# A decoder layer's split token rows, key rows and fourth weight pool at other places modulo 256 bytes

## The chip, the core and the metric

The kernel runs on one core of a Trainium2 chip. The core has a matrix engine (TensorE, "PE" in the profile, with its weight loads on a row of their own, "PEld"), a vector engine (VectorE, DVE), a scalar engine (ScalarE, ACT), a general engine (GpSimd, POOL) and a queue engine that issues transfers (SyncE, SP). The on-chip memory (SBUF) has 128 partitions; an address in this document is a byte offset within a partition. The metric is the device time of one execution in microseconds; the median of several runs is compared.

## What is computed

One decoder layer over 4096 prompt tokens and 64 sample tokens, width 1024, in float32. It has one input projection, three head groups and one output projection:

```python
h = _rmsnorm(x, g_pre)
z = h @ w_in                                    # 1024 x 2816
cb, cc, ch, cg, q, k, v, ag, mq, mg = _split_cols(z)
out_a = silu(cg) * cb * conv3(cc * ch)          # gated short convolution, 256 channels
out_b = silu(ag) * window_attention(q, k, v, sink)   # 8 heads, window 128
out_c = silu(mg) * memory_attention(mq, mk, mv)      # 4 heads, 256 memory tokens
y = concatenate([out_a, out_b, out_c]) @ w_out
return x + _rmsnorm(y, g_post)
```

Keys, values, convolution rows and memory keys and values are outputs too.

## The kernel before

**Products in parts.** The matrix unit multiplies in a reduced-width float32 form (float32r). To keep float32 accuracy each operand is split: `hi` is the operand rounded to that form, `lo` the remainder. A product is then three matmuls, weights-hi times rows-hi, weights-hi times rows-lo, weights-lo times rows-hi. `product` (L368) does this for four slices of 128 inputs, so twelve matmuls of line 373 per product, each with a stationary 128 x 128 slice `w[:, 0 or 1, ks]` and a moving row of 260 tokens, `h[0][:, k]` (hi) or `h[1][:, k]` (lo).

**The input projection.** The 4160 token rows are cut into 8 blocks of 2 x 260 tokens (`NBLK`, `HW`). Blocks are done with Strassen-like products, seven per 2 x 2 partition (`PRODUCTS`), apart from the first two of the first phase, which are done plainly with eight (`plain_block`). There are three phases (`PHASES`), with four pairs of weight columns in the first two and three in the last. `input_projection` (L924) runs over `steps` = (phase, block, product); while one step multiplies, `h_split(i + 1)` prepares the next rows: `split` (L361) writes the hi tile with ScalarE (L363) and the lo tile with VectorE (L364). Accumulators in PSUM are evicted by `evict` (L376 to L395), mostly on VectorE at L380. In the trace the plain blocks and phase 0 last to about 350 us, phase 1 to about 670, phase 2 to about 926, and window and memory attention with the output projection from there to the end.

**Order.** Phase 0 is under a manual schedule; in the later phases the program order is kept for chosen instructions. Matmuls run in program order on TensorE.

**Where tiles lie.** Tiles come from pools on a left stack that grows up and a right stack that grows down. For this document the residue modulo 256 counts, and the sizes below are bytes per partition. In the program of before the pools start at:

| pool | holds | address | modulo 256 |
|---|---|---|---|
| `wa` | weights of pairs 0 to 2, later `w_out` and the split `mix` | 20,704 | 224 |
| `wb` (right) | weights of pair 3 in phases 0 and 1 | 200,672 | 224 |
| `hp` | two hi and two lo tiles | 131,680 | 96 |
| `bq` | queries of even chunks | 115,040 | 96 |
| `keys` | keys of even chunks (`kst`) | 147,808 | 96 |
| `pre` (right) | queries of odd chunks, then their keys | 195,744 | 160 |
| `memkv` (right) | memory keys `mk` first | 215,200 | 160 |

A weight tile takes 4096 bytes (parts 2048 apart, slices 512 apart). A split tile takes `KH` = 4 rows with a pitch of `XR` = 320 elements, 1280 bytes, so 5120 in all; 260 of the 320 elements are used, and `begins` (L354) says at which element the used part starts: 48 for hi and 16 for lo. Hence hi rows start at 96 + 192 = 288, place 32, and lo rows at 96 + 64, place 160, in every tile.

In attention `kst` has four rows of 384 elements (1536 bytes) per chunk of 256 tokens, hi and lo of two key heads, and `mk` has two parts of 1024 elements. Line 1253 multiplies queries (stationary) with `kst` (moving, 256 columns), line 1189 queries with `mk`, and line 1499 the split `mix` (stationary) with `w_out` (moving, 512 columns, in `wa` too; the last block's second half has 256).

Steps that the change and the working touch: `begins` and `split_tile` (L354 to L359), `wb` (L87), `place` (L90), `third_start` (L731: `mk`, `mrows`), `input_projection` (L924), `open_attention` (L1012), `load_keys` (L1108), `sample_window` (L1374).

Of the kernel before, what the change touches and what calls it, by code (L numbers as in the profile page):

```python
# [8 lines left out]
F32 = mybir.dt.float32  # L9
F32R = mybir.dt.float32r  # L10
# [5 lines left out]
P = 128  # L16
# [6 lines left out]
NT = 4096 + NS  # L23
HW = 260
XR = 320
NBLK = NT // (2 * HW)
CT = 256
NCH = 4096 // CT
# [14 lines left out]

PHASES = (((8, 9), (14, 15), (16, 17), (12, 13)), ((0, 1), (2, 3), (4, 5), (6, 7)), ((10, 11), (18, 19), (20, 21)))
PLAIN_BLOCKS = 2


def f(ap):
    return ap.bitcast(F32)
# [3 lines left out]
def hybrid_layer(ctx: ExitStack, tc: tile.TileContext, a: dict):  # L53
# [30 lines left out]
    wa = ctx.enter_context(tc.tile_pool(name="wa", bufs=3 * NP_))  # L84
    pa = ExitStack()
    wb_stack = ExitStack()
    wb = wb_stack.enter_context(tc.tile_pool(name="wb", bufs=NP_, side="right"))  # L87
    psa = ExitStack()

    place = ctx.enter_context(tc.tile_pool(name="place", bufs=1)).tile([P, 2, KH, HW], F32, name="place")  # L90
    hxp = pa.enter_context(tc.tile_pool(name="hx", bufs=4))
    hp = pa.enter_context(tc.tile_pool(name="hp", bufs=2))
    own = ExitStack()
# [257 lines left out]
                tc.keep_in_program_order(ins)  # L351
            store(hd[b][o], ops[o])

    begins = {"hi": 48, "lo": 16}  # L354

    def split_tile(tag, name):

        n = begins[tag]
        return hp.tile([P, KH, XR], F32R, tag=tag, name=name)[:, :, n : n + HW]  # L359

    def split(src, name):  # L361
# [343 lines left out]
    idle = accumulator(1, 2, "idle")  # L705
    warm = hp.tile([P, KH, XR], F32R, tag="lo", name="warm").rearrange("p k n -> p (k n)")
    G.memset(f(warm[:, : P + 512]), 1.0)
# [18 lines left out]
    right = ctx.enter_context(ExitStack())  # L726
    mem_stack = ExitStack()
    mss = const.tile([P, 4], F32, name="mss")
    third = {}

    def third_start():  # L731
        keep = right.enter_context(tc.tile_pool(name="memkv", bufs=1, side="right"))
        third["mk"] = keep.tile([P, 2, 4, 256], F32R, name="mk")
        third["mkv"] = keep.tile([P, 2, 512], F32, name="mkv")

        third["vt"] = keep.tile([P, P], F32, name="vt")
        sink, nsink = (keep.tile([P, 8], F32, name=n) for n in ("sink", "nsink"))
        third["sink"], third["nsink"] = sink, nsink
        wmask = third["wmask"] = keep.tile([P, 2, P], U8, name="wmask")
        negs = third["negs"] = keep.tile([P, 2, P], F32, name="negs")  # L740
        tc.keep_in_program_order(DMA.dma_start(sink, a["sinks"].partition_broadcast(P)))
        V.tensor_scalar(nsink, sink, -1.0, None, op0=ALU.mult)
        tc.keep_in_program_order(DMA.dma_start(negs, a["wmask"]))
        G.tensor_copy(wmask, negs)  # L744
        G.memset(negs, NEG)
        third["pre"] = right.enter_context(tc.tile_pool(name="pre", bufs=1, side="right"))

        third["parts"] = third["pre"].tile([P, 12, CT], F32, tag="q", name="mparts").rearrange("p (a b) n -> p a (b n)", a=6)
        third["mrows"] = third["pre"].tile([P, 4, P + CT], F32, tag="k", name="mrows").rearrange("p a n -> p (a n)")
        third["mem"] = mem_stack.enter_context(tc.tile_pool(name="mem", bufs=3, side="right"))  # L750
        tc.keep_in_program_order(DMA.dma_start(gmem, a["gmem"]))

# [169 lines left out]
        DMA.dma_start(third["gpost"], a["gpost"].partition_broadcast(P))  # L922

    def input_projection():  # L924
        for i, (ph, b, p) in enumerate(steps):
            if ph > 0 and b == 0 and p == 0:
                h_split(i + 1)
                for fn in pending.pop(i, ()):
                    fn()
                flush()  # L930
                in_order.close()
                store_queue[0] = DMA
                own.close()
                if ph == 2:
                    kept_z.close()
                    wb_stack.close()
                open_phase(ph)
                if ph == 2:
                    third_start()
            quads = range(len(PHASES[ph]))  # L940
            flush()
            h_load(i + 3)
            if ph == 0 or b > 0 or p > 0:
                h_split(i + 1)
            jobs = list(pending.pop(i, ()))
            if ph < 2 and p < 3:
                jobs.insert(0, lambda: t_sum(ph, b, f"T{p + 2}"))
            if ph < 2:
                jobs += next_block(ph, b, p)
            if (ph, b, p) == (0, last, 2):  # L950
                jobs.append(us_load)
            if ph == 2:
                jobs += third_jobs(b, p)
            if (ph, b) in sums_at and p in (2, 3, 4):
                jobs.append(lambda pair=sums_at[ph, b], k=p - 2: w_sums(pair, k, sums_to[pair]))
            if i > 0 and steps[i - 1][0] == 1 and steps[i - 1][1] == NBLK - 1:

                o = PRODUCTS[steps[i - 1][2]][0]
                for q in range(len(PHASES[2])):
                    load, fill = lambda q=q, o=o: next_load(2, q, o), lambda q=q, o=o: next_fill(2, q, o)  # L960
                    if o in ("S4", "A22"):

                        pending.setdefault(i + 1, []).append(load)
                        pending.setdefault(i + 3, []).append(fill)
                    else:
                        jobs.append(load)
                        pending.setdefault(i + 1, []).append(fill)
            if ph == 2 and b == last:
                for j in ((0, 1, 2), (3, 4), (5, 6, 7), (8, 9, 10, 11), (12, 13, 14, 15), (), ())[p]:
                    jobs.append(lambda j=j: wo_load(j))  # L970
                    pending.setdefault(i + (3 if j in (10, 11) else 2), []).append(lambda j=j: wo_split(j))
                if p == 1:
                    pending.setdefault(i + 1, []).append(gains_load)
                if p == 4:
                    jobs.append(blocks[0].split)
            if (ph, b, p) in SWITCH:
                jobs = SWITCH[ph, b, p]() + jobs
            if p == 0:
                zz[b] = [[None, None] for _ in quads[::2]]
            done = 0  # L980
            for q in quads:
                w = min(2, len(quads) - q // 2 * 2)
                if q % 2 == 0:
                    if p < 2:
                        zz[b][q // 2][1 - p] = z_tile(w, f"z{ph}_{b}_{q}_{1 - p}")
                    acc = accumulator(i, w, f"c{ph}_{b}_{q}_{p}")
                product(ws[ph, q, PRODUCTS[p][0]], hs[i], acc[:, q % 2])
                if q % 2 == w - 1:
                    evict(p, acc, *zz[b][q // 2])
                upto = len(jobs) * (q + 1) // len(quads)  # L990
                for fn in jobs[done:upto]:
                    fn()
                done = upto
            mem_sum()
            if p == NP_ - 1:
                z_done((0, 2, 1, 3) if ph == 1 else (2, 3, 0, 1) if ph == 0 else (1, 0))
            if p >= 5:
                ends = finish(ph, b, zz[b], p - 5)
                now = 2 if ph == 0 and b < NBLK - 1 else 1 if ph == 1 and b == 0 else len(ends)
                pending.setdefault(i + 1, []).extend(ends[:now])  # L1000
                pending.setdefault(i + 2, []).extend(ends[now:])
        for i in sorted(pending):
            for fn in pending[i]:
                fn()
        flush()
# [6 lines left out]
    def open_attention():  # L1012
# [8 lines left out]
              for tag in ("s", "t", "z", "pv")}  # L1021
# [2 lines left out]
        bq = att.enter_context(tc.tile_pool(name="bq", bufs=1))  # L1024
        places = {tag: att.enter_context(tc.tile_pool(name=tag, bufs=1 if tag == "yn" else 2))
                  for tag in ("sm", "p", "yn", "pt", "pv")}
        keys = att.enter_context(tc.tile_pool(name="keys", bufs=1))
        places["xpt"] = att.enter_context(tc.tile_pool(name="xpt", bufs=2))
        bp = {"k": keys, "vT": att.enter_context(tc.tile_pool(name="vT", bufs=1)), "q": bq}
# [9 lines left out]
    att = ctx.enter_context(ExitStack())  # L1039
# [57 lines left out]
    class Chunk:  # L1097
# [10 lines left out]
        def load_keys(self):  # L1108
            c, t0 = self.c, self.t0

            self.kst = self.pool("k").tile([P, 4, P + CT], F32R, tag="k", name=f"kst{c}")
            lo = P if c == 0 else 0
            if c == 0:
                G.memset(f(self.kst[:, :, 0:P]), 0.0)
# [258 lines left out]

    def sample_window():  # L1374
        zs = third["zs"]
        keys = bp["k"].tile([P, 4, P + CT], F32, tag="k", name="skc").rearrange("p a n -> p (a n)")
        kc = keys[:, : NB * P].rearrange("p (b k) -> p b k", b=NB)
        qb = keys[:, NB * P :].rearrange("p (b c) -> p b c", b=NB)
        DMA.dma_start(kc, a["cwk"])
# [9 lines left out]
        G.memset(neg, NEG)  # L1389
        tc.keep_in_program_order(V.tensor_scalar(scol[:, 1:2], scol[:, 0:1], -1.0, None, op0=ALU.mult))  # L1390
        yield
        values = third["pre"].tile([P, 4, P + CT], F32, tag="k", name="svc").rearrange("p a n -> p (a n)")
        vc = values[:, : NB * P].rearrange("p (b k) -> p b k", b=NB)
        DMA.dma_start(vc, a["cwv"])
        vn = vp.tile([P, P], F32, tag="v", name="svn")[:64]
# [294 lines left out]
```

## Time and profile before

| | |
|---|---|
| median of 3 runs | 1532.0 us (1529.85 to 1535.95) |
| profiled execution | 1529.03 us |
| its span, first to last instruction | 1527.3 us |
| granted TensorE clock | 1.00 |
| PE busy | 1514.2 us (99%) |
| DVE, ACT, POOL busy | 75%, 53%, 25% |

The page's fourth part follows the work that ended last back to the start:

```profile
PE 87%; DVE 5%; issue 4%; DMA 2%; POOL 1%; ACT 1%; SPq 0%; ACTq 0%; POOLq 0%; DVEq 0%
PE c L373 47%; PE y L1499 23%; PE ws L1253 4%; PE wo L1095 2%; PE wt L1276 2%; PE xs L1189 2%; PE xt L1204 2%; PE wo L1225 2%; PE wo L1231 1%; PE mem_acc L796 1%; DVE z L380 1%; DMA ws10A<-in_w_in 1%; DMA vd<-v 1%; DMA place<-hd_B 0%; DMA ws20A<-in_w_in 0%
```

In such rows "c" is an accumulator, L373 the line, and the share is that of the span. A timeline row has its start in us, its length, engine, line, operation, tiles (written tile, arrow, read tiles), the shape and a count where like instructions are merged. In tile names digits of phase and block are partly left out: `hi_6B` is a hi tile of a block 6, `w_3S` a weight tile of pair 3.

### The profile page before, as it was taken

Reading aid. Unit: us, or ns where it says so; the run is one execution under the profiler, and the core shown is the slowest. Engines: PE = TensorE matmul, PEld = TensorE weight load, DVE = VectorE, ACT = ScalarE, POOL = GpSimd, SP = SyncE. Lnnn points to the kernel's source line nnn. Section 1 sums busy time; section 2 is a strip of 40 time slices with the busy share of each in tenths; the row PEclk is TensorE's granted clock in tenths of the full one; section 3 lists DMA queues with packets and bytes.
Section 4 is the critical chain, followed back from the end, with each engine's and each line's share of the span. In section 5 each row is a group of like instructions: output and inputs, shape, how many; then the busy total and the mean of one; then the engine's idle time right before and its main releaser. Section 6 shows DMA issues by size and latency. Waiting matters only on the chain.

```text
span 1527.3 us, 30150 instructions
## 1 busy us (share of the span) xinstructions
PE 1514.2 (99%) x11331; PEld 1391.6 (91%) x11331; DVE 1145.1 (75%) x2055; ACT 806.2 (53%) x2039; POOL 381.0 (25%) x604
## 2 busy tenths in 40 slices
PE   9999999999999999999999999999999999999998
PEld 9999999999999999999999998788888888888876
DVE  6778888899887777997677678766666666666743
ACT  7776666576222222445455457656655565565632
POOL 0222333221300000000101204544444444444310
PEclk9999999999999999999999999999999999999999
DMA  9989999878755333778877789977777777776333
GB/s 274 200 213 242 286 277 259 301 238 273 194 182 181 127 127 127 240 231 278 243 262 224 242 286 259 226 160 149 149 148 152 162 149 158 162 155 145 131 110 97
DMA packets 177943, 306.28 MB, mean 201 GB/s; under 512 B 33926, under 2 KB 107654, under 8 KB 177766
## 3 DMA queue, kind: packets, MB, share of 16 engines
q1 hardware_dynamic: 130901, 227.38, 48.2%
q0 software_dynamic: 46176, 75.92, 24.9%
q8 instruction: 90, 1.47, 0.4%
q10 hardware_dynamic: 720, 1.05, 0.2%
q14 instruction: 56, 0.45, 0.1%
HBM read 197.23 MB, written 108.05 MB: 200 GB/s over the span
## 4 chain that ended last, share of the span: by engine, by line
PE 87%; DVE 5%; issue 4%; DMA 2%; POOL 1%; ACT 1%; SPq 0%; ACTq 0%; POOLq 0%; DVEq 0%
PE c L373 47%; PE y L1499 23%; PE ws L1253 4%; PE wo L1095 2%; PE wt L1276 2%; PE xs L1189 2%; PE xt L1204 2%; PE wo L1225 2%; PE wo L1231 1%; PE mem_acc L796 1%; DVE z L380 1%; DMA ws10A<-in_w_in 1%; DMA vd<-v 1%; DMA place<-hd_B 0%; DMA ws20A<-in_w_in 0%
## 5 line engine op out<-in xcount | busy, mean ns | idle before, releaser
L1499 PE MATMUL y<-wo,mh 128*128 128x512 f32 (+1 forms) x1040 | 350.1, 399 | 0.0
L380 DVE TENSOR_TENSOR z<-c,z 128x520 f32<-128x520 f32 (+1 forms) x308 | 194.8, 647 | 80.7 <-PE c L373 79.0
L1499 PEld LDWEIGHTS y<-wo,mh 128*128 128x128 f32 x1040 | 194.3, 188 | 39.3 <-issue 2.4
L1499 PE MATMUL y<-wo,ml 128*128 128x512 f32 (+1 forms) x520 | 201.8, 388 | 0.0
L1266 ACT ACTIVATE sm<-sm,wnm 128x128 f32<-128x128 f32 x256 | 99.5, 390 | 60.9 <-DVE wnm L1260 60.0
L1198 POOL TENSOR_SCALAR xp<-xp,xrd 128x256 f32<-128x256 f32 x128 | 74.6, 590 | 208.0 <-DVE xrd L1194 207.1
L1499 PEld LDWEIGHTS y<-wo,ml 128*128 128x128 f32 x520 | 98.2, 189 | 16.2
L1190 DVE TENSOR_REDUCE xmx<-xs 128x2 f32<-128x512 f32 x64 | 44.1, 689 | 59.3 <-PE xs L1189 59.2
L1278 ACT COPY wpt<-wt 128x512 f32<-128x512 f32 x64 | 37.2, 582 | 87.7 <-PE wt L1276 85.2
L1253 PEld LDWEIGHTS ws<-kst,q 128*128 128x128 f32 x512 | 70.0, 190 | 5.4 <-ACT xp L1193 0.7
L1506 DVE TENSOR_TENSOR yn<-y,gpost 128x512 f32<-128x512 f32 (+1 forms) x66 | 45.1, 684 | 39.6 <-PE y L1499 39.3
L1253 PE MATMUL ws<-kst,q 128*128 128x256 f32 x512 | 73.1, 283 | 0.4 <-ACT xp L1193 0.4
L1507 ACT ACTIVATE y<-y 128x512 f32<-128x512 f32 (+1 forms) x66 | 38.5, 584 | 64.2 <-DVE yn L1506 64.2
L744 POOL CAST wmask<-negs 128x256 uint8<-128x256 f32 x1 | 0.8, 822 | 265.2 <-ACT z L382 265.2
L1286 POOL TENSOR_SCALAR_AFFINE_SELECT wpt<-wpt 128x512 f32<-128x512 f32 x64 | 52.7, 823 | 42.0 <-ACT wpt L1278 39.1
L1193 ACT ACTIVATE xp<-xs,xnm 128x256 f32<-128x256 f32 x128 | 58.9, 464 | 7.1 <-DVE xnm L1191 7.1
L1128 POOL DMA_DIRECT2D q<-qd x64 | 42.8, 674 | 70.2 <-DMA qd<-zh 60.2
L1117 POOL DMA_DIRECT2D kst<-qd x64 | 38.7, 617 | 63.7 <-PE xt L1204 41.5
L1517 DVE SCALAR_TENSOR_TENSOR xr<-yn,yst,xr 128x1024 f32<-128x1024 f32 (+2 forms) x34 | 43.1, 1269 | 14.6 <-POOL yst L1513 13.2
L1256 DVE COPY_PREDICATED sm<-wmask,ws 128x256 f32<-128x256 uint8 x124 | 52.1, 436 | 2.4 <-ACT sm L1255 2.0
L1283 POOL TENSOR_SCALAR_AFFINE_SELECT wpv<-wpt 128x512 f32<-128x512 f32 x62 | 40.5, 653 | 50.6 <-ACT wpt L1278 50.5
L275 ACT ACTIVATE nat<-nat 104x1024 f32<-104x1024 f32 x40 | 42.3, 1057 | 18.5 <-DMA nat<-in_x_p 18.5
(962 smaller groups left out, 5076.2 us busy)
## 6 DMA issues: line engine op xcount, KB each, us to landing
q<-qd POOLq DMA_DIRECT2D x64, 384.0 KB, 8.3
xr<-in_x_p SPq DMA_DIRECT2D x32, 512.0 KB
nat<-in_x_p SPq DMA_DIRECT2D x39, 416.0 KB
o_yp<-xr SPq DMA_DIRECT2D x31, 512.0 KB
md<-th POOLq DMA_DIRECT2D x48, 260.0 KB, 7.2
qd<-zh SPq DMA_DIRECT2D x48, 260.0 KB
qd<-z SPq DMA_DIRECT2D x48, 260.0 KB
kst<-qd POOLq DMA_DIRECT2D x60, 192.0 KB, 5.5
```

Of the source, the lines that this page charges most:

```text
L373: TE.matmul(bank[:, :HW], l, r, start=first and i == 0, stop=last and i == 3 * KH - 1)
L380: add = lambda dst, other: V.tensor_tensor(dst, c, other, op=ALU.add)
L1190: V.tensor_reduce(mx[:, :nb], s, axis=AX.X, op=ALU.max)
L1193: S.activation(p[:, i, :], s[:, i, :], AF.Exp, bias=nm[:, i : i + 1], scale=SCALE, accum_out=den[:, i : i + 1])
L1198: G.tensor_scalar(p[:, i, :], p[:, i, :], rd[:, i : i + 1], 0.5, op0=ALU.mult, op1=ALU.mult)
L1253: TE.matmul(s3[:, hh, :], self.q[:, 4 + 2 * (2 * half + hh) + kvh, i * P : i * P + P], self.kst[:, 2 * kvh + part, i * P : i * P + 2 * P], ...
L1256: V.copy_predicated(sm[:, 2 * half : 2 * half + 2, :], third["wmask"], third["negs"] if first else s3[:, :, 0:P])
L1266: S.activation(sm[:, hh, :], sm[:, hh, :], AF.Exp, bias=nm[:, hh : hh + 1], scale=SCALE, accum_out=den[:, hh : hh + 1])
L1286: G.affine_select(p3, p3, pattern=[[0, 4], [1, P]], compare_op=ALU.is_ge, fill=0.0, base=0, channel_multiplier=-1)
L1499: TE.matmul(acc, self.hl[l][:, k], wo[k][c0 // 512][:, r, c0 % 512 : c0 % 512 + c1 - c0], start=j == 0, stop=j == passes * KT - 1)
L1506: V.tensor_tensor(yn[:m, c0:c1], acc[:m], gpost[:m, c0:c1], op=ALU.mult)
L1517: V.scalar_tensor_tensor(self.xr[:m, cs], yn[:m, cs], st[:m, 3:4], self.xr[:m, cs], op0=ALU.mult, op1=ALU.add)
```

## The change

- `begins` is no longer fixed. `PLACES` gives, for each phase and each half of the eight blocks, two pairs of begins (hi, lo), and `split_tile` takes them by turns: a counter per tag, odd calls take the second pair and even calls the first. `input_projection` sets the pairs at the first step of block 0 and of block 4 of each phase; the plain blocks have those of phase 0.
- A padding tile of 16 elements (64 bytes) goes on the right stack ahead of `wb`, so `wb` starts 64 bytes lower.
- `kst` and the tiles that share its slots get a pitch of `KR` = 416 elements (1664 bytes) where 384 were; users of the flat tile take its first 1536 elements.
- `mk` gets 32 elements more per part, so its second part starts 4224 bytes after the first.
- Padding tiles of 16 elements go ahead of the keys, in `pre` and, by a helper `pad`, in front of `keys`.

Worked out from the table above, places after the change: begins 0, 16, 32, 48 give 96, 160, 224, 32; `wa` stays at 224; `wb` at 160. `mk` starts 256 bytes lower, at 160, its second part at 32. `pre` starts 832 bytes lower, at 96, its keys at 160. `keys` starts at 160. Successive rows of `kst` alternate between 160 and 32.

| blocks | odd calls: hi, lo at | even calls: hi, lo at |
|---|---|---|
| plain, phase 0 | 96, 160 | 224, 32 |
| phase 1 | 96, 224 | 224, 160 |
| phase 2, blocks 0 to 3 | 96, 32 | 224, 96 |
| phase 2, blocks 4 to 7 | 32, 160 | 160, 96 |

```diff
+KR = 416
+PLACES = ((((32, 48), (0, 16)), ((32, 48), (0, 16))), (((32, 16), (0, 32)), ((32, 16), (0, 32))), (((32, 0), (0, 48)), ((16, 0), (48, 16))))
...
     wb_stack = ExitStack()
+    wb_stack.enter_context(tc.tile_pool(name="padw", bufs=1, side="right")).tile([P, 16], F32, name="padw")
     wb = wb_stack.enter_context(tc.tile_pool(name="wb", bufs=NP_, side="right"))
...
+    def pad(where, n, side="left"):
+
+        pads[0] += 1
+        where.enter_context(tc.tile_pool(name=f"pad{pads[0]}", bufs=1, side=side)).tile([P, n], F32, name=f"pad{pads[0]}")
...
-    begins = {"hi": 48, "lo": 16}
+    begins, turn = PLACES[0][0], {"hi": 0, "lo": 0}

     def split_tile(tag, name):

-        n = begins[tag]
+        turn[tag] += 1
+        n = begins[turn[tag] % 2][tag == "lo"]
         return hp.tile([P, KH, XR], F32R, tag=tag, name=name)[:, :, n : n + HW]
...
-        third["mk"] = keep.tile([P, 2, 4, 256], F32R, name="mk")
+        third["mk"] = keep.tile([P, 2, 4 * 256 + 32], F32R, name="mk")[:, :, : 4 * 256].rearrange("p a (h k) -> p a h k", k=256)
...
-        third["mrows"] = third["pre"].tile([P, 4, P + CT], F32, tag="k", name="mrows").rearrange("p a n -> p (a n)")
+        third["pre"].tile([P, 16], F32, tag="pad", name="padk")
+        third["mrows"] = third["pre"].tile([P, 4, KR], F32, tag="k", name="mrows").rearrange("p a n -> p (a n)")
...
     def input_projection():
+        nonlocal begins
         for i, (ph, b, p) in enumerate(steps):
+            if b in (0, NBLK // 2) and p == 0:
+                begins = PLACES[ph][b > 0]
...
+        pad(att, 16)
         keys = att.enter_context(tc.tile_pool(name="keys", bufs=1))
...
-            self.kst = self.pool("k").tile([P, 4, P + CT], F32R, tag="k", name=f"kst{c}")
+            self.kst = self.pool("k").tile([P, 4, KR], F32R, tag="k", name=f"kst{c}")[:, :, : P + CT]
```

The tiles `skc` and `svc` in `sample_window` get the pitch `KR` in the same way.

More of the change, by code (lines that the diff above doesn't have):

```diff
@@ L90, in hybrid_layer @@
     place = ctx.enter_context(tc.tile_pool(name="place", bufs=1)).tile([P, 2, KH, HW], F32, name="place")
+    pads = [0]
+    def pad(where, n, side="left"):
+        pads[0] += 1
+        where.enter_context(tc.tile_pool(name=f"pad{pads[0]}", bufs=1, side=side)).tile([P, n], F32, name=f"pad{pads[0]}")
     hxp = pa.enter_context(tc.tile_pool(name="hx", bufs=4))
@@ L1375, in sample_window @@
         zs = third["zs"]
-        keys = bp["k"].tile([P, 4, P + CT], F32, tag="k", name="skc").rearrange("p a n -> p (a n)")
+        keys = bp["k"].tile([P, 4, KR], F32, tag="k", name="skc").rearrange("p a n -> p (a n)")[:, : 4 * (P + CT)]
         kc = keys[:, : NB * P].rearrange("p (b k) -> p b k", b=NB)
@@ L1391, in sample_window @@
         yield
-        values = third["pre"].tile([P, 4, P + CT], F32, tag="k", name="svc").rearrange("p a n -> p (a n)")
+        values = third["pre"].tile([P, 4, KR], F32, tag="k", name="svc").rearrange("p a n -> p (a n)")[:, : 4 * (P + CT)]
         vc = values[:, : NB * P].rearrange("p (b k) -> p b k", b=NB)
```

## The prediction

> **What bounds the kernel now.** I read the page first, then the waits of TensorE, then the stages (the windows view, line 373 alone), and last the timeline of single matmuls.
>
> ```profile
> span 1527.3 us, 30150 instructions
> PE 1514.2 (99%) x11331; PEld 1391.6 (91%) x11331; DVE 1145.1 (75%) x2055; ACT 806.2 (53%) x2039; POOL 381.0 (25%) x604
> ...
> L380 DVE TENSOR_TENSOR z<-c,z 128x520 f32<-128x520 f32 (+1 forms) x308 | 194.8, 647 | 80.7 <-PE c L373 79.0
> ```
>
> TensorE works for 1514.2 of 1527.3 us, so no more than 13 us of waiting is left. The evictions of line 380 wait for it (79.0 of their 80.7 idle us), not the reverse. Whatever lengthens or shortens a matmul therefore passes into the span nearly one to one.
>
> ```profile
> core 0: us, PE busy (x) PEld busy (x), PEclk, DMA share, GB/s
> 0.00:113.00 113.00, 105.91 (x881) 104.90 (x882) 1.00 0.92 231
> 113.00:350.00 237.00, 236.22 (x2004) 235.80 (x2002) 1.00 0.93 268
> 350.00:670.00 320.00, 318.22 (x2694) 317.60 (x2695) 1.00 0.54 177
> 670.00:926.00 256.00, 232.86 (x1915) 228.96 (x1913) 1.00 0.78 255
> ```
>
> Up to 926 us nearly everything is line 373, its 7488 matmuls, at a granted clock of 1.00 throughout. Busy time cannot show what I need, since these durations overlap. The number that counts is the **step**, from the start of one matmul to the start of the next, and the timeline has it:
>
> ```profile
> 611.40 0.70 DVE L444 SCALAR_TENSOR_TENSOR z<-cth,z 128x520 f32<-128x520 f32 x1 [0.71 <-ACT cth L443]
> ...
> 612.03 0.28 PE L373 MATMUL c<-lo_6B,w_3S 128*128 128x260 f32 x1
> 612.03 0.30 PEld L373 LDWEIGHTS c<-hi_6B,w_3S 128*128 128x128 f32 x2
> 612.14 0.40 PE L373 MATMUL c<-hi_6B,w_3S 128*128 128x260 f32 x2
> 612.26 0.19 PEld L373 LDWEIGHTS c<-lo_6B,w_3S 128*128 128x128 f32 x1
> 612.38 0.28 PE L373 MATMUL c<-lo_6B,w_3S 128*128 128x260 f32 x1
> ...
> 612.86 1.06 ACT L363 CAST hi_7B<-x_7B 128x1040 fp32r<-128x1040 f32 x1 [1.49 <-PE c L373]
> ...
> 613.09 0.28 PE L373 MATMUL c<-lo_6T,w_0A 128*128 128x260 f32 x1
> ...
> 613.44 0.28 PE L373 MATMUL c<-lo_6T,w_0A 128*128 128x260 f32 x1
> ```
>
> Two things stand there. The load of the next weights starts with the running matmul (both at 612.03), so each step is a moving read of 260 columns beside a stationary read of 128. And three matmuls take 0.35 us with ScalarE idle (612.03 to 612.38) and 0.35 us while it writes the next hi tile (613.09 to 613.44): the other engines' traffic does not show, the two reads of TensorE itself may.
>
> **What the places are.** I call *place* a byte address modulo 256, and *distance* the place of the moving row minus the place of the weights that are loaded meanwhile. From the pools' start addresses (in the section on the kernel) weights lie at 224, hi rows at 32, lo rows at 160. All pitches on this path (512, 1280, 2048, 4096, 5120 bytes) are multiples of 256, so before the change every hi matmul has distance 64 and every lo matmul 192.
>
> ```profile
> 5.68 0.59 PE L373 MATMUL c<-hi_0B,w_0A 128*128 128x260 f32 x1
> 6.06 0.42 PE L373 MATMUL c<-lo_0B,w_0A 128*128 128x260 f32 x1
> ...
> 922.83 0.28 PE L373 MATMUL c<-lo_7T,w_2A 128*128 128x260 f32 x1
> 922.94 0.28 PE L373 MATMUL c<-hi_7T,w_2A 128*128 128x260 f32 x1
> ```
>
> Between these rows, by the starts in the trace, steps of line 373 (those more than 12 ns over the median, 37 in all, left out) average **118.85 ns** over 4930 hi and **116.02 ns** over 2486 lo. Distances 0 and 128 do not occur in line 373, so they must be bounded from other lines.
>
> ```profile
> 775.90 1.11 PE L1253 MATMUL ws<-kst,q 128*128 128x256 f32 x8
> 1442.34 1.00 PE L1253 MATMUL ws<-kst,q 128*128 128x256 f32 x7
> 801.27 0.64 PE L1189 MATMUL xs<-mk,q 128*128 128x256 f32 x4
> 1452.93 0.63 PE L1189 MATMUL xs<-mk,q 128*128 128x256 f32 x4
> 1515.26 0.28 PE L1499 MATMUL y<-wo,ml 128*128 128x256 f32 x1
> 1520.78 0.28 PE L1499 MATMUL y<-wo,mh 128*128 128x256 f32 x1
> ```
>
> *Distance 0, 256 columns:* line 1253 119.11 ns (435 steps), line 1189 in odd chunks 117.56 (107), the last block of line 1499 119.85 (47); weighted 118.9. Line 1189 in even chunks has distance 64 and takes 118.54 (83 steps, from 954.73 to the row at 1414.76 below).
>
> ```profile
> 924.02 0.39 PE L1499 MATMUL y<-wo,mh 128*128 128x512 f32 x1
> 930.63 0.39 PE L1499 MATMUL y<-wo,mh 128*128 128x512 f32 x1
> 948.41 0.62 PE L1499 MATMUL y<-wo,mh 128*128 128x512 f32 x2
> 954.73 0.72 PE L1189 MATMUL xs<-mk,q 128*128 128x256 f32 x4
> 1414.53 0.40 PE L1499 MATMUL y<-wo,mh 128*128 128x512 f32 x1
> 1414.76 0.64 PE L1189 MATMUL xs<-mk,q 128*128 128x256 f32 x4
> 1452.70 0.39 PE L1499 MATMUL y<-wo,mh 128*128 128x512 f32 x1
> 1514.92 0.50 PE L1499 MATMUL y<-wo,mh 128*128 128x512 f32 x2
> ```
>
> *512 columns, line 1499:* distance 0 between 924.02 and 1514.92, 229.69 ns (1256 steps). Where the next weights are those of a query, the same code has distance 64 in odd chunks (930.63 to 1452.70), 226.15 ns over 60 steps, and 128 in even ones (948.87 less one step, to 1414.53), 232.28 ns over 54. This is the cleanest pair: only the place differs.
>
> A column costs (226.15 - 118.54) / 256 = 0.42 ns, so four more make 1.7 ns: **distance 0 at 260 columns 118.9 + 1.7 = 120.6** (119.3 to 121.6 by its three rows). At 512 columns distance 0 lies 3.5 ns over 64, at 260 columns 1.75 over 118.85: half shows. Half of 128's 6.1 is 3.05: **distance 128 = 121.9**. Its bounds are 116.0 (nothing excludes that it is as good as 192) and 125.0 (all 6.1). I take the middle one, nearest to the rows with a like load beside them.
>
> **The change, part by part.**
> *Split tiles.* With hp's start at place 96, begins of 0, 16, 32, 48 give 96, 160, 224, 32. The padding tile ahead of wb moves the fourth pair's weights (phases 0 and 1) from 224 to 160; wa stays. Half of each phase's matmuls have each parity; two thirds are hi; a quarter use wb in phases 0 and 1. Over plain blocks and phase 0 (2784 matmuls), phase 1 (2688) and each half of phase 2 (1008), counted by distance:
>
> - distance 0: 2268 (before 0)
> - distance 64: 1420 (before 4992)
> - distance 128: 2156 (before 0)
> - distance 192: 1644 (before 2496)
>
> Sum: 2268 x 120.6 + 2156 x 121.9 - 3572 x 118.85 - 852 x 116.02 ns = 536.3 - 523.4 = **+13.0 us**. No instruction is added; ScalarE and VectorE write the same tiles at other addresses, and at 53% and 75% busy, beside the matmuls, they hide what that could cost. Were it not hidden: there are 154 splits, and 20 ns each (the spread of one, 1.046 to 1.070 us in the row below) make 3 us.
>
> ```profile
> L363 ACT CAST hi_2T<-x_2T x8: 1046/1063/1070, 108.1 to 748.5; 128x1040 fp32r<-128x1040 f32 x8
> ```
>
> *Attention.* The pitch of 416 columns and the pads put queries at 96 and keys at 160 and 32 by turns: line 1253 goes from distance 0 to 64 and 192. The longer memory keys do the same to line 1189. At 256 columns 64 costs about 117.6 (between 117.15, from line 373, and 118.54) and 192 114.3 (116.02 - 1.7), mean 116: 512 x (119.1 - 116) + 256 x (118.05 - 116) = -2.1 us. Where line 1499 is followed by a query's weights, 60 steps go from distance 64 to 128, +0.4. Other tiles behind the pads shift too, but their matmuls are plain fp32 products and transposes, whose steps are the same at every place that they have. Net -1.7 (0 to -3). Pools shift by under 1 KB; no wait is added.
>
> **Sum:** +13.0 - 1.7 = +11.3 us, on the profiled execution's 1529.03 us 1540.3. That execution is 3.0 us under the median of the three runs (1532.0), against which I forecast **1543 us**.
>
> **The rivals.**
> *The place does not matter.* The 2.8 ns between hi and lo may come from the position in the triple (lo is followed by other weights, w[:,1]) and not from 64 against 192; line 373 cannot part the two. For it: line 1189 at distance 64 is 1 ns slower than at 0, against my order. Against it: the pair 226.15 and 232.28. Time 1532 less up to 2. The Trainium skill is on this side: "SBUF — State Buffer", section "Who interferes with whom", has it that PE never waits on anyone, and "TensorE: Matmul & The Clock Gate", "Step-by-step: what each phase is for", that loading the next weights takes no read bandwidth from the running matmul. By it the change gives 0 us; the pair above speaks against it, and its gap for a warm matmul ("Back-to-back issue gap", 260 columns: 110.8 ns as an estimate) lies under both of this trace's means, 116.02 and 118.85. Chance 0.30.
>
> *Faster: at 260 columns 0 and 128 behave like 192.* The 512-column rows have a weights load beside their first half alone; with 260 columns the two reads end nearly together, and the order could turn over. At 116.0 for both, 4424 x 116.0 - 523.4 = -10.2, with attention -12: 1520 us. The point from which it decides: the mean of the two distances under 523.4 / 4424 = 118.3 ns. Only this trace's lack of such rows speaks for it; the three distance-0 rows (119.3 or more) speak against half of it. Chance 0.13.
>
> *The full penalty.* 125.0 at 128 and 121.6 at 0 give +21.9 - 1.7: 1552 us. Chance 0.07.
>
> **How the numbers follow.** My forecast has 0.50; 0.07 of that ends under +0.5%, which is about what a measurement of this kernel can tell from no change. Slower: 0.43 + 0.07 = 0.50; same: 0.30 + 0.07 = 0.37; faster: 0.13. The range 1526 to 1553 holds the unknown distances' upper bounds and the case without effect (1530 to 1532, with 4 us for the spread of runs); it leaves out most of the faster case. The likeliest case alone: 1536 to 1549.
>
> **What would show it.** In the timeline after, steps of line 373 grouped by phase and parity: 119 and 116 where the pair is (64, 192), in the second half of phase 2; 120 to 122 for hi in its first half, in both parities. The stage from 350 to 670 us should grow by about 5 us, the second half of phase 2 by nothing, attention should shrink by about 2. If all phases keep 118.85 and 116.02, places do not matter; if hi in phase 0 falls under 118, I have the order of the distances wrong.

## The result and the profile after

The changed kernel takes **1540.61 us** (median of 8 runs, 1538.93 to 1542.45) against 1532.37 before (8 runs). The ratio is 1.0057, with a 95% interval of 1.0045 to 1.0069, so it is slower by about 8.7 us. The profiled execution took 1540.83 us (1529.03 before). All steps and windows below come from one profiled execution of each kernel.

The page after, its first lines and the group of evictions (engine, busy us and share, count; then line, engine, operation, tiles, shapes, count, busy us, mean ns, idle us before them and what ended it):

```profile
span 1539.1 us, 30149 instructions
...
PE 1527.2 (99%) x11331; PEld 1404.9 (91%) x11331; DVE 1146.2 (74%) x2055; ACT 805.1 (52%) x2039; POOL 381.7 (25%) x604
...
L391 DVE TENSOR_TENSOR z<-c,z 128x520 f32<-128x520 f32 (+1 forms) x308 | 194.5, 644 | 91.1 <-PE c L384 89.6
```

There is as much work as before, with the same counts on TensorE. TensorE is busy 13.0 us longer and the span is 11.8 us longer. VectorE and ScalarE are busy for the same time within 1.1 us, and the evictions wait 10.6 us longer for the projection's matmuls (89.6 us against 79.0). So the matmuls themselves take longer. The stages show where. Below are the windows of the projection's line alone, between the starts of plain blocks, phase 0, phase 1, phase 2 and the end of phase 2, first before, then after; the third number is the stage's length, the fourth TensorE's busy time in it:

```profile
0.00:99.10 99.10, 92.38 (x768) 91.58 (x769) 1.00 0.94 240
99.10:337.20 238.10, 237.73 (x2018) 237.52 (x2017) 1.00 0.93 261
337.20:657.80 320.60, 318.04 (x2690) 317.00 (x2689) 1.00 0.55 181
657.80:923.10 265.30, 244.94 (x2018) 241.16 (x2016) 1.00 0.77 251
```

```profile
0.00:102.10 102.10, 93.78 (x768) 92.58 (x769) 1.00 0.94 230
102.10:344.20 242.10, 241.96 (x2019) 241.76 (x2018) 1.00 0.93 258
344.20:668.00 323.80, 323.57 (x2690) 323.06 (x2690) 1.00 0.55 180
668.00:936.60 268.60, 248.25 (x2018) 244.18 (x2016) 1.00 0.77 249
```

Every stage of the projection loses, by 1.4, 4.2, 5.5 and 3.3 us of busy time. In phase 1 the stage grew by only 3.2 of its 5.5 us. Before, TensorE stood idle there for 320.60 - 318.04 = 2.6 us, mostly for lo tiles of line 364; after, for 0.2. Slower matmuls give the splits time to finish. The plain blocks grew by 3.0 us, of which only 1.4 are busy time. The rest is waiting at the start that is not clearly the change's: in e1_attention_alone below, whose projection is that of before, phase 0 also starts 2.0 us later than before.

Three matmuls of one slice make a *triple*: weights-hi with hi rows, weights-hi with lo rows, weights-lo with hi rows. The table gives the steps (start to start) of each of the three by the *pair* (distance of hi, distance of lo) of the tile, and their mean. They come from the starts in the trace. Left out are steps 12 ns or more over the median of their group, and the steps in which the next weights lie at another place (from the third to the fourth weight pair and from the fourth to the first):

| pair | triples | hi | lo | hi again | mean ns |
|---|---|---|---|---|---|
| (64,192), before | 2494 | 118.6 | 116.0 | 119.1 | 117.9 |
| (64,192) | 156 | 119.3 | 116.8 | 119.1 | 118.4 |
| (0,64) | 348 | 119.1 | 117.0 | 119.8 | 118.6 |
| (128,64) | 166 | 119.1 | 120.5 | 119.4 | 119.7 |
| (0,192) | 336 | 119.5 | 118.8 | 121.3 | 119.9 |
| (0,128) | 168 | 120.0 | 118.4 | 121.3 | 119.9 |
| (128,192) | 360 | 125.1 | 116.3 | 118.8 | 120.1 |
| (64,0) | 112 | 119.4 | 121.7 | 119.7 | 120.3 |
| (192,64) | 108 | 122.0 | 117.4 | 121.5 | 120.3 |
| (128,0) | 336 | 119.9 | 120.6 | 120.5 | 120.3 |
| (192,128) | 168 | 122.8 | 118.0 | 122.4 | 121.1 |
| (64,128) | 116 | 120.0 | 122.5 | 121.4 | 121.3 |
| (192,0) | 120 | 122.1 | 120.0 | 122.2 | 121.4 |

The change puts all twelve pairs with two different distances into the projection, and the one from before is the best of them. Line by line over the whole trace, with waits taken apart: the projection's 7488 steps sum to 897.9 us against 883.0 (+14.9), lines 1253, 1499 and 1189 of before lose 1.1, 0.9 and 0.2 us, and the waits fall by 1.3.

The change also moves the places that ScalarE and VectorE write. That is not what slows the matmuls: in phase 0 of the changed kernel the steps that start while a split is being written average 119.75 ns, the others 119.93 (before, 117.78 and 117.79).

### The profile page after: what moved, and what is told of

It reads as the page before. It is cut to its first block, busy times and chain, and to the rows that moved or that the text cites. A ratio compares the mean times of both kernels' runs of the same rounds, so it can differ in the third digit from the quotient of the medians.

```text
span 1539.1 us, 30149 instructions
## 1 busy us (share of the span) xinstructions
PE 1527.2 (99%) x11331; PEld 1404.9 (91%) x11331; DVE 1146.2 (74%) x2055; ACT 805.1 (52%) x2039; POOL 381.7 (25%) x604
## 4 chain that ended last, share of the span: by engine, by line
PE 87%; DMA 6%; DVE 3%; ACT 2%; issue 1%; POOL 0%; ACTq 0%; SPq 0%; DVEq 0%; POOLq 0%
PE c L384 49%; PE y L1515 22%; PE ws L1269 4%; PE wo L1111 2%; DMA nat<-in_x_p 2%; PE wt L1292 2%; PE xs L1205 2%; PE xt L1220 2%; PE wo L1241 2%; PE wo L1247 1%; DMA x_0B<-in_xt 1%; PE mem_acc L808 1%; DMA qd<-z 1%; DMA wr_2A<-in_w_in 1%; DMA md<-th 0%
## 5 line engine op out<-in xcount | busy, mean ns | idle before, releaser
L391 DVE TENSOR_TENSOR z<-c,z 128x520 f32<-128x520 f32 (+1 forms) x308 | 194.5, 644 | 91.1 <-PE c L384 89.6
L393 ACT COPY z<-c 128x520 f32<-128x520 f32 (+1 forms) x44 | 24.4, 554 | 53.4 <-PE c L384 50.8
```

The costliest lines, as they stand in the source:

```text
L391: add = lambda dst, other: V.tensor_tensor(dst, c, other, op=ALU.add)
```

## Experiments

All start from the kernel before. Ratios are to that kernel, run beside them. Of e4 to e7 and e9 there is one run each; these are read for their steps and not for their time.

### The two parts alone

*e1_attention_alone* has the hunks of the change that concern attention:

```diff
-            self.kst = self.pool("k").tile([P, 4, P + CT], F32R, tag="k", name=f"kst{c}")
+            self.kst = self.pool("k").tile([P, 4, KR], F32R, tag="k", name=f"kst{c}")[:, :, : P + CT]
...
-        third["mk"] = keep.tile([P, 2, 4, 256], F32R, name="mk")
+        third["mk"] = keep.tile([P, 2, 4 * 256 + 32], F32R, name="mk")[:, :, : 4 * 256].rearrange("p a (h k) -> p a h k", k=256)
...
+        pad(att, 16)
```

> The attention part of the change alone (pitch 416 of the key rows, longer memory keys, pads ahead of the keys); split tiles and the fourth weight pool stay where they were. Theory A (the two parts of the change are independent and add up): line 1253 falls from 119.1 to 117.1 ns a step and the memory-key line by 0.2 us in all, as in the changed kernel, so 1 to 2 us less than before, ratio 0.999; line 373 keeps 118.85 (hi) and 116.02 (lo). Rival B (the pools behind the pads now start waits or collide elsewhere): not faster than before, 1532 or more.

Measured: 1529.39 us, ratio 0.9984 (0.9973 to 0.9995). The keys' line sums to 60.0 us against 61.1, the output projection's to 359.9 against 360.8, and the projection's steps stay as they were (883.5 us). The attention part is a small gain of about 2.4 us, and the interval holds theory A's 0.999. Among the kernels with several runs this one has the lowest ratio.

The traces of this run and of the changed kernel also repeat the prediction's cleanest pair as an experiment. Line 1499's 60 steps beside which a query's weights are loaded, in odd chunks, go from distance 64 to 128 because the queries moved, and from 226.15 to 232.6 ns in e1 (232.7 in the changed kernel). The same steps in even chunks, where nothing moved, stay at 232.3 to 232.4. The other steps of this line fell by 1.0 ns (229.7 to 228.7) although neither their rows nor their weights moved; why, no run shows.

*e2_projection_alone* has the other hunks: `PLACES`, its use in `split_tile` and `input_projection`, and the pad ahead of `wb`.

> The places of the split tiles and the pad ahead of the fourth weight pool alone; attention as before. Theory A: line 373 sums to 14 to 15 us more than before, as in the changed kernel (883 to 898 us), so the time is 1 to 2 us above the changed kernel's 1540.6: 1542, ratio 1.006 to 1.008. Rival B (some of the loss came from attention's pads): under 1540, ratio under 1.005.

Measured: 1539.76 us, ratio 1.0060 (1.0048 to 1.0073), the steps of the projection 897.3 us. The ratio, at the lower end, and the steps are as theory A has them. The time is under theory A's 1542, and just under rival B's 1540, because the kernel before ran at 1530.64 beside it and not at 1532.37; the ratio is over the rival's 1.005, though the interval reaches under it. The loss is that of the projection; 0.9984 x 1.0060 = 1.0044 is within the error of the whole change's 1.0057.

### Distance or place

*e3_all_shifted* moves everything by 64 bytes modulo 256 and so keeps all distances:

```diff
+    ctx.enter_context(tc.tile_pool(name="padl", bufs=1)).tile([P, 16], F32, name="padl")
+    ctx.enter_context(tc.tile_pool(name="padr", bufs=1, side="right")).tile([P, 48], F32, name="padr")
     const = ctx.enter_context(tc.tile_pool(name="const", bufs=1))
```

> The kernel before with everything in SBUF 64 bytes further modulo 256 (a pad at the bottom of each stack): all places differ, all distances between moving rows and weights stay. Theory 'distance': steps of line 373 stay at 118.85 (hi) and 116.02 (lo), time 1532, ratio 0.999 to 1.001. Rival 'absolute place' (a place of its own is good or bad): weights now lie at 32, hi rows at 96 and lo rows at 224; in the changed kernel hi rows at 96 averaged 120 to 125 and lo rows at 224 120.6, so line 373 grows by 10 us or more, 1542.

Measured: 1530.43 us, ratio 0.9995 (0.9986 to 1.0004). The projection's steps sum to 882.9 us, hi and lo at 118.9 and 116.0. Its windows, over the same stages as before:

```profile
99.10:337.20 238.10, 237.73 (x2019) 237.52 (x2018) 1.00 0.92 261
337.20:657.80 320.60, 318.62 (x2696) 317.60 (x2695) 1.00 0.54 182
657.80:923.10 265.30, 244.81 (x2016) 240.91 (x2014) 1.00 0.77 251
```

In phase 0's window TensorE is busy for 237.73 us, the same to the second decimal, with every SBUF address in it at another place. So no place was good or bad by itself under this shift of 64 bytes. That the place of the weights counts, and not only that of the rows among themselves, is seen in the changed kernel: in phase 0 the even tiles' rows (224 and 32) take 118.7 ns a step with weights at 224, pair (0,64), and 121.1 with those of the fourth pair at 160, pair (64,128). In the kernel before, where both weight pools lie at 224, the fourth pair's steps are the same as the others', 117.8 ns in phases 0 and 1.

### Own distance or pair

*e4_pairs* gives each phase, half and parity a pair of its own, with `wb` not padded:

```diff
+PLACES = ((((32, 32), (48, 48)), ((0, 0), (16, 16))), (((48, 16), (16, 48)), ((48, 32), (48, 0))), (((0, 16), (16, 0)), ((0, 32), (48, 16))))
...
-        n = begins[tag]
+        turn[tag] += 1
+        n = begins[turn[tag] % 2][tag == "lo"]
```

> The kernel before with twelve pairs (distance of hi, distance of lo), one for each phase, half and parity, all weights at 224: (0,0), (64,64), (128,128), (192,192), (64,192) twice, (192,64), (64,0), (64,128), (128,192), (192,128), (128,0). Theory 'own distance' (a step depends on its own matmul's distance alone, as in the prediction, with the changed kernel's averages 120.2, 119.0, 120.35, 119.7 for 0, 64, 128, 192): means of three of 120.2, 119.0, 120.35, 119.7 for the equal pairs, 119.2 for (64,192) and 119.3 for (192,64). Theory 'pair' (hi and lo distance together set all three steps): the pairs known from before and the changed kernel come back at their means of three, (64,192) 117.9, (192,64) 120.3, (64,0) 120.3, (64,128) 121.3, (128,192) 120.05, (192,128) 121.1, (128,0) 120.3, the last four of these now from other phases or pools; equal pairs unknown, 118 to 122. If a pair's mean differs by over 0.5 between phases or between weights at 160 and at 224, neither holds.

Measured (one run, 1541.11 us): (0,0) 118.7, (64,64) 120.0, (128,128) 120.1, (192,192) 119.9. Theory "own distance", the prediction's, falls: it had 120.2 for (0,0) and 119.0 for (64,64); the other two equal pairs are within 0.3 of it. Five known pairs came back within 0.3 at other places and in other phases: (192,64) 120.6, (64,0) 120.0, (64,128) 121.1, (128,192) 120.0, (128,0) 120.3. But (192,128) took 119.3 where the changed kernel had 121.1, and (64,192), 117.9 before, took 119.5 in phase 1, where it came by turns with (192,64), and 118.5 in phase 2, by turns with (128,0). So "pair" is not the whole either.

The rows of one product tell why. These are the first and the last lo matmul of the same product of phase 1 (block 2, weights S4 with rows B22, 16 triples, so 15 between the rows), with hi rows at 32, lo rows at 160 and weights at 224 in both kernels; first before, then e4_pairs:

```profile
447.13 0.28 PE L373 MATMUL c<-lo_2B,w_0S 128*128 128x260 f32 x1
...
452.43 0.28 PE L373 MATMUL c<-lo_2B,w_3S 128*128 128x260 f32 x1
```

```profile
453.43 0.28 PE L375 MATMUL c<-lo_2B,w_0S 128*128 128x260 f32 x1
...
458.83 0.28 PE L375 MATMUL c<-lo_2B,w_3S 128*128 128x260 f32 x1
```

5.30 us and 5.40 us: triples of 353.3 and of 360.0 ns, from the same code on the same addresses. Step by step the first repeats 118, 116, 119 (119 for 118 in every third triple) and the second, from its second triple on, 123, 118, 119. What differs by the edit is the product ahead of it, with pair (64,192) in the first kernel and (192,64) in the second. This gave a new theory: the matmuls settle into a repeating cycle of three steps, a pair has one or more such cycles, and how it is entered decides which.

### Settled cycles

*e5_uniform_a* (first line below) and *e6_uniform_b* (second line) have one pair per half of a phase, the same for both parities. *e7_sixteen* and *e9_scan*, not shown, change the same line, with begins in steps of 4 elements, 16 bytes:

```diff
+PLACES = ((((32, 48), (32, 48)), ((48, 16), (48, 16))), (((0, 16), (0, 16)), ((48, 16), (48, 16))), (((32, 32), (32, 32)), ((48, 16), (48, 16))))
```

```diff
+PLACES = ((((16, 48), (16, 48)), ((16, 16), (16, 16))), (((0, 48), (0, 48)), ((48, 48), (48, 48))), (((32, 16), (32, 16)), ((16, 0), (16, 0))))
```

> The kernel before with one pair (distance of hi, of lo) per half of a phase, both parities alike: plain blocks and first half of phase 0 (0,64), second half (64,192); phase 1 (128,192), then (64,192); phase 2 (0,0), then (64,192). Theory 'pair' (a pair has one cost): the three (64,192) halves come back at 117.9 each, (0,64) 118.6, (128,192) 120.0, (0,0) 118.7. Theory 'settled cycle' (the steps of a pair settle to a repeating cycle of three, and some pairs have more than one; which one it falls into depends on how it is entered, and it then stays): within a (64,192) half nearly all triples are of one kind, either 118/116/119 (117.8) or 122/119/119 (119.8), and (0,64), without the change of parity, stays in its cycle 119/115/119 or 120/115/119 (117.8 or less) instead of 118.6; (0,0) about 118.7.

> As the run before it in the list, with (192,64), (192,192), (128,64), (64,64), (0,192), (192,128) in the six halves. Theory 'pair': 120.4, 119.85, 119.65 (119.0 to 119.65 so far), 119.97, 119.9, and 119.3 to 121.1 for the last. Theory 'settled cycle': without the change of parity each stays in a cycle, so the spread of its triples' sums within a half falls to 1 or 2 ns, and means may lie up to 1 ns under those.

Measured (one run each, 1534.02 and 1541.72 us, one run of the kernel before beside them 1536.29), mean step over the triples of the stage: (64,192) in phases 0 and 1 117.8 twice; in the second half of phase 2, where attention's first chunk comes between, 118.4. (0,64) 117.8 in phase 0; (0,0) 118.75; (128,64) 118.9; (0,192) 119.8; (192,192) 120.0; (64,64) 120.0, 430 of its 432 triples in phase 1 being 120, 120, 120; (192,128) 120.3; (192,64) 120.7; (128,192) 122.1. Theory "settled cycle" gets the form right for half of the ten pairs: for (64,192), (0,64), (128,192), (64,64) and (192,192) nearly all triples of a stage have the same sum within 1 ns, apart from (64,192) in phase 2. It does not for (0,0), (192,64), (128,64), (0,192) and (192,128), which go through several kinds of triple by turns. And the new cycle of (128,192) is worse than the 120.0 that the pair had in e4_pairs, not better by up to 1 ns. In e5_uniform_a, first (128,192), then (64,192), rows again 15 triples apart:

```profile
450.21 0.28 PE L375 MATMUL c<-lo_2B,w_0S 128*128 128x260 f32 x1
...
455.71 0.28 PE L375 MATMUL c<-lo_2B,w_3S 128*128 128x260 f32 x1
...
571.08 0.28 PE L375 MATMUL c<-lo_5B,w_0S 128*128 128x260 f32 x1
...
576.38 0.28 PE L375 MATMUL c<-lo_5B,w_3S 128*128 128x260 f32 x1
```

5.50 us against 5.30: 366.7 and 353.3 ns a triple, within one kernel and at the same granted clock.

> The kernel before with pairs 16 bytes apart, one per half of a phase: (64,192), (80,192), (48,192), (64,208), (64,176), (80,208). If only the 64-byte part of a place counts, all are 117.8 or the second cycle's 119.8. If the distance counts finely, the means differ by more than 0.5 from both and (80,208), with both moved alike, need not equal (64,192); one under 117 would be worth a whole kernel (1 ns a step is 7.5 us).

Measured (one run, 1539.70 us): (80,192) 120.0, (48,192) 119.8, (64,208) 120.0, (64,176) 119.0; (80,208) 118.2, most of its triples at 353. So 16 bytes count, and here one row moved alone loses the good cycle.

> Six more uniform pairs at 16-byte places: (16,80), (0,80), (0,48), (96,224), (32,160), (16,144). So far triples settle near 353.3, 360.0 or 366.7 ns (117.8, 120.0, 122.2 a step) or wander between. If pairs shifted together by 16 bytes keep their cycle, as (64,192) and (80,208) did, (16,80) is at 117.8 as (0,64) is, and (96,224) and (32,160) at 117.8 to 118.3; with one row moved alone, (0,80) and (0,48), 119 to 120 as (80,192) and (48,192). A triple under 353 would be a new cycle, 346.7 by the spacing of the three, worth 16 us over the whole kernel.

Measured (one run, 1539.94 us): (16,80) 120.0, (0,80) 120.0, (0,48) 118.2, (96,224) 120.6, (32,160) 120.0, (16,144) 120.0. The idea that pairs moved together keep their cycle fell: it held for (80,208), not for (16,80), (96,224) or (32,160). Its other half fell too: (0,48), with one row moved alone from (0,64), took 118.2 and not 119 to 120. No pair settled under 353.3.

### Is it the turn from pair to pair?

*e8_alternate* changes the pair at every tile, but between pairs that are good when uniform:

```diff
+PLACES = ((((48, 16), (32, 48)), ((48, 16), (32, 48))), (((48, 16), (52, 20)), ((32, 48), (32, 32))), (((48, 16), (48, 16)), ((48, 16), (48, 16))))
```

> Change of pair at every tile, but only between pairs that are good when they are uniform: plain blocks and phase 0 (64,192) and (0,64) by turns, first half of phase 1 (64,192) and (80,208), second half (0,64) and (0,0), phase 2 (64,192) throughout. Theory 'pair' (each pair brings its own cost, turns cost nothing): 117.8 to 117.9 in phases 0 and 1a, 118.3 in 1b, time within 2 us of before, ratio 1.000 to 1.002. Theory 'turns cost' (every change of pair has to settle anew, some 12 to 48 matmuls at 119 to 122): 118.4 to 119.0 in the alternating stages, 4 to 8 us more than before, ratio 1.003 to 1.005.

Measured: 1531.40 us, ratio 1.0013 (1.0004 to 1.0023). Steps average 118.1 in phases 0 and 1a (the first half of phase 1) and 118.6 in 1b (the second), the projection sums to 885.3 us. Both means lie 0.3 ns over theory "pair", between the two theories; the time is the one of "pair". Over the 5472 steps of these stages 0.3 ns is 1.6 us of the 2.3 us that the projection has more than before; the rest is (0,0), which takes about 118.7 by itself. A tile's first matmuls settle (for (0,64) in the changed kernel the steps begin 119, 120, 124, 121, 121, 123, 120, 120, 122, 118, and after some twenty they repeat 119, 115, 119), the rest is the pair's own. Of the change's +14.9 us the turns can therefore explain a smaller part. That the pairs themselves make the larger one is borne out by the seven of the twelve that e5 and e6 ran uniform: at their uniform means, their 1644 triples in the changed kernel would take 9.1 us more than at 117.9 ns a step, and they take 8.6 us more. Single pairs differ, though, (128,192) most with 122.1 against 120.1.

## Why the prediction came out as it did

**The bound and the kind of effect were right.** TensorE's steps set the time, no other engine's did; they change with the place of the rows relative to the weights; and the sum was +14.9 us for +13.0 forecast in the projection and -2.2 for -1.7 in attention. e1 and e2 part the two as forecast. That both sums came out so near is in part luck, as the next two paragraphs show.

**The rule behind the four terms was wrong.** The prediction gave each matmul a cost by its own distance. The terms, with the prediction's counts, against what the changed kernel has, averaged over each distance:

| distance | matmuls | predicted ns | measured ns | error of the sum |
|---|---|---|---|---|
| 0 | 2268 | 120.6 | 120.2 | -0.9 us |
| 64 | 1420 | 118.85 | 119.0 | +0.2 us |
| 128 | 2156 | 121.9 | 120.35 | -3.3 us |
| 192 | 1644 | 116.02 | 119.7 | +6.1 us |

Two large errors, -3.3 and +6.1 us, nearly cancel, which is luck. 192 was mis-sized most. The 116.0 of the lo rows before is not the price of distance 192: hi rows at 192 take about 122 in the changed kernel's three pairs. It is one step of the cycle that (64,192) settles into. The first rival had named the weak spot, that line 373 cannot part the distance from the position in the triple. For 128 the step that failed is scaling the 512-column rows' 6.1 ns by a half; at 260 columns 128 is within 0.2 ns of 0, though at 512 columns the 6.1 ns came again in e1.

**Attention's sum was right by other terms.** Lines 1253 and 1189 were to gain 2.1 us together, at a mean of 116 ns a step; they gained 1.3, at 117.1 and 117.5. The 60 steps of line 1499 cost the forecast 0.4. What filled the gap is 1.3 us less in the other steps of line 1499, which the prediction did not have.

**Waits.** That TensorE had 13 us of waiting left and would pass a loss on nearly one to one was right within 1.3 us between the two profiled executions. The loss hid most of phase 1's waits for lo tiles, and the wait at the start grew.

**The rivals.** "The place does not matter" is out: the same code takes 117.8 and 122.1 ns a step in two stages of e5_uniform_a. Its reason, the position in the triple, does not explain the 2.8 ns between hi and lo either: in (64,64), where both have the same distance, all three positions take 120.0. The rule of the Trainium skill ("TensorE: Matmul & The Clock Gate", "Step-by-step: what each phase is for") has it that loading the next weights takes no read bandwidth from the running matmul. The traces do not agree with the 0 us that the prediction drew from it: the projection's steps grew by 14.9 us, and the measurement decides; that it is these two reads that collide was not tried by itself. "Faster" is out as well: it needed a mean of 0 and 128 under 118.3 ns and they have 120.3, and no pair tried at 16- or 64-byte steps settles under 117.8. "The full penalty" needed 125.0 at distance 128, and it has 120.35.

**The time.** 1543 was 2.4 us too high. The sum on the profiled execution, 1540.3, was close to the 1540.83 of the profiled execution after. The 3.0 us added for the median account for the excess. The kernel before kept that median (1532.37 over eight runs, 3.3 us over its profiled execution), but the median after is 0.2 us under its own profiled execution. So the medians lie only 8.2 us apart where the profiled executions lie 11.8 apart. In later groups of runs the kernel before had medians of 1530.64 and 1529.77; why its runs lie so much over its profiled execution in one group and not in others is not shown.

**The signs.** Phase 1 was to grow by about 5 us; its busy time grew by 5.5, but the stage by 3.2, the rest being waits that went. The second half of phase 2 was to grow by nothing; its steps grew by 1.4 us (119.28 to 120.72 us over 1008 matmuls), since (192,128) took 121.1 and not 118. Hi rows in the first half of phase 2 were to take 120 to 122 in both parities; they do with (0,128), and with (128,64) they take 119.1 to 119.4.

What stays open is the rule that leads from a pair to its cycles. The runs show which pairs are good, not why, and which access waits for which was not tried by itself. That only the address modulo 256 counts was taken for granted; what the runs show for it is that the four slices of a product, whose rows lie 768 bytes further from their weights each time, take the same (353.3 to 353.4 ns a triple each in phase 0 before).

## What to carry to other kernels

Where matmuls follow each other densely, each with its own weights load, measure start-to-start steps and not durations, and group them by the place modulo 256 of the moving row relative to the weights: 3.7% lay between the best and the worst pair here (117.8 and 122.1 ns). Do not give a price to each operand by itself; try whole combinations, each for a whole stage and each at its own steady sequence, and then keep one combination throughout. Several combinations can share one run, a stage for each, so a scan costs little.

## What the runs showed of the hardware

- Where triples settle into one kind, their sums are near 353.3, 360.0 and 366.7 ns, 6.7 ns apart, at a granted clock of 1.00 for the stage.
- The same product on the same addresses ran at 353.3 ns a triple in one kernel and at 360.0 in another with other matmuls ahead of it, and kept that from its second triple to its last.
- A move of 16 bytes of one operand can cost as much as one of 64: from (64,192) with 117.8 ns a step, (80,192) goes to 120.0 and (0,192) to 119.8.
- With 512 moving columns, other weights to be loaded next, at 64 bytes from their old place, took the step from 226.15 to 232.6 ns (line 1499, 60 steps, e1_attention_alone).
